# Windowed attention: the products with the values of one group are made together one group later, the output projection in half portions, TensorE held to the written order

## The chip, the cores and the metric

The kernel runs on one core of one Trainium2 chip. The metric is device time in microseconds (us) of one execution. The time before is the median of three runs; a profiled execution of the same kernel gives the trace that every reading below comes from. A difference under 0.3% (about 9 us) can't be told from no change here.

## What is computed

Two layers over 1024 latent tokens with 256 context tokens ahead of them, model width 1024. Layer 0 mixes tokens by two recurrent head groups, layer 1 by windowed attention; each layer ends with an MLP. Only the attention of layer 1 is touched by the change:

```python
def window_attention(q, k, v, k_c, v_c, sink):
    # q: 16 heads x 1024 x 64; k, v: 4 heads x 1024 x 64; k_c, v_c: 4 heads x 256 x 64
    ...
    s_loc = jnp.einsum('bkgnqd,bkncd->bkgnqc', qb, kb) * scale   # 128 queries x 3 blocks of 128 keys, band of +-128
    s_ctx = jnp.einsum('bkgnqd,bkld->bkgnql', qb, k_c) * scale   # the same queries x 256 context keys
    m = max over s_loc, s_ctx and the head's sink
    e_loc, e_ctx = jnp.exp(s_loc - m), jnp.exp(s_ctx - m)
    denom = sum(e_loc) + sum(e_ctx) + jnp.exp(s_sink - m)
    return (e_loc @ vb + e_ctx @ v_c) / denom
...
y = merge_heads(window_attention(...)) @ od_w_out
x = layer_norm(alpha * x + gate * y)
```

## The kernel before

The attention of layer 1 is cut into 32 groups: 8 blocks of 128 queries (`n`) by 4 key heads (`g`), with the 4 query heads of a key head worked on together. A group has `nk` blocks of 128 keys: 3 of the window and 2 of the context (at `n` = 0 and 7 one less). The closures of `group(n, g)` are its steps:

- `scores(i)`, i = 0 to 3, one query head: five matmuls into a score tile (`pS`, 2 buffers), then VectorE takes the maximum (`tensor_reduce`), scales it (`tensor_scalar`), and ScalarE makes the exponentials `E` (6 buffers) with their sum.
- `turn(kk)`, one block of keys: TensorE transposes that block of the four `E` into `pE` (2 buffers), ScalarE (VectorE for kk = 2) copies it to `Et`.
- `pv(kk)`: the product of that `Et` with 64 columns of the values, summed over kk in `pO` (1 buffer). The stationary side has 64 columns, and the two halves of `pO`'s partitions are written in turn.
- `dens()`: one over the denominators, and GpSimd's diagonal tiles `dg` from them. `end()`: a product of `dg` with ones in `pO`'s other half (so that every row gets its denominator), then VectorE and ScalarE make `yf`, and from it `yh` and `yl`, the two parts in which the output is kept.

Beside that runs `rest`, a chain of generators: after every second block of queries, `residual` multiplies the output of 256 tokens by the output weights (`w_out_steps`: 8 steps, each 24 matmuls into `pW` with one weight tile `w`), adds it to the residual stream and makes the layer norm. A `w` is made by `wsplit`: a load of 512 KB, a rounding copy on ScalarE (`hi`), a subtraction on GpSimd (`lo`); the pool `wg` holds 5 of them. `adv(rest, 1)` asks for one step.

A scheduler sets the order on each engine from the written order and a model of times. It may move an instruction ahead of others that are written earlier; once the program is built, every engine works strictly in the order it was given.

The loop over the groups, in which group u+1's scores are made during group u:

Of the kernel before, what the change touches and what calls it, by code (L numbers as in the profile page):

```python
# [9 lines left out]
F32 = mybir.dt.float32  # L10
# [9 lines left out]
P = 128  # L20
KT = 8
T = 1280
NT = 10
# [6 lines left out]
def chunk_of(t):  # L30
    return 0 if t < 2 else (1 if t < 6 else 2)
# [3 lines left out]
def backbone(ctx: ExitStack, tc: tile.TileContext, xT, cin, wmod, bmod, lng, lnb, w1, w2,  # L35
             wfm, wlr, wv, theta, gkw, gkb, normg, wo0, wq, wkv, sink, wo1, cst, rst, rope, out,
             stop=None, dbg=None):
    nc = tc.nc
# [3 lines left out]
            kw["reuse_waits"] = "tile"  # L42
        return tc.tile_pool(**kw)

    V, S, G, TE, SY = nc.vector, nc.scalar, nc.gpsimd, nc.tensor, nc.sync

    cp = ctx.enter_context(pool(name="cp", bufs=1))
    cp.tile([P, 16], F32, tag="pad", name="pad")
# [8 lines left out]
    def nm(s):  # L57
        uid[0] += 1
        return f"{s}_{uid[0]}"
# [104 lines left out]
    def chain(*gens):  # L164
        for g_ in gens:
            yield from g_
# [9 lines left out]
    def reserve(pool, tags):  # L176

        for tag, shape, dt, nb in tags:
            for _ in range(nb):
                pool.tile([P] + shape, dt, tag=tag, name=nm(tag), bufs=nb)  # L180
# [18 lines left out]
    def mm3(pt, wh, wl, xh, xl, start, stop):  # L199
        TE.matmul(pt, lhsT=wh, rhs=xh, start=start, stop=False)  # L200
        TE.matmul(pt, lhsT=wh, rhs=xl, start=False, stop=False)  # L201
        TE.matmul(pt, lhsT=wl, rhs=xh, start=False, stop=stop)  # L202
# [19 lines left out]
    wp = es_b1.enter_context(pool(name="w_b1", bufs=3, side="right"))  # L222
# [99 lines left out]
    with es_b1:  # L322
# [20 lines left out]
        for q in range(4):  # L343
# [5 lines left out]
            for a in range(2):  # L349
                k = 2 * q + a  # L350
# [33 lines left out]
        E = {}  # L384
# [101 lines left out]
    wg = ctx.enter_context(pool(name="wg", bufs=5, side="right"))  # L486
    with pool(name="b2", bufs=1) as b2:
# [38 lines left out]
        order = [1, 0] + list(range(9, 1, -1))  # L526
# [7 lines left out]
        for oi, t in enumerate(order):  # L534
            ci = chunk_of(t)
            j = cj(ci)
# [143 lines left out]
        for _ in w_out_steps(*a):  # L680
            pass

    def w_out_steps(y, wsrc, wp, acc, l, j, pW, engs=(None, None), wnext=None):

        n = acc.shape[2]
        yh, yl = y
        for u in range(KT):
            wh, wl = [w.rearrange("p (k m) -> p k m", k=KT) for w in (wnext() if wnext else wsplit(wp, wsrc[u], engs[u % 2]))]
            pt = pW()
            for k in range(KT):  # L690
                xh, xl = [y_[k // 4][:, k % 4, :] if isinstance(y_, list) else y_[:, k, :] for y_ in (yh, yl)]
                mm3(pt[:, :n], wh[:, k, :], wl[:, k, :], xh, xl, k == 0, k == KT - 1)
            V.scalar_tensor_tensor(acc[:, u, :], pt[:, :n], gta[:, l, 0, u, j:j + 1], acc[:, u, :],  # L693
                                   op0=ALU.mult, op1=ALU.add)
            yield
# [15 lines left out]
    with pool(name="b3", bufs=1) as b3:  # L711
# [28 lines left out]
        order = [wfm] + [wfm] + [wo0, wfm] * 3 + [wo0, wo0]  # L740
# [497 lines left out]
    yall = [hy.tile([P, KT, 512], F32R, tag=f"y{i}", name=f"y{i}") for i in "hl"]  # L1238
    with pool(name="p2", bufs=1) as p2:
        vts = {}  # L1240
        reserve(p2, [("E", [640], F32, 6), ("vc", [256], F32, 2), ("vl", [256], F32, 4)])

        def get_v(t):
            if t not in vts:
# [9 lines left out]
        def residual(y, t, ci):  # L1254
            o0 = (t - 1) * P - CH[ci][0]
            if o0 == 0:
                accs[ci] = new_acc(acp, ci)
            asl = accs[ci][:, :, o0:o0 + 256]
            G.tensor_copy(asl[:, 0, 0:1], first[0])
            SY.dma_start(asl, xd[ci][:, :, o0:o0 + 256])  # L1260
            yield from w_out_steps(y, wo1, wg, asl, 1, 0, pW if t < NT - 1 else pE, (None, None) if t < NT - 1 else (None, V))
            if t in (NT - 3, NT - 1):
                make_h(accs[1][:, :, o0:o0 + 256], 1, 1, 0, *[y_[:, :, o0:o0 + 256] for y_ in yall], p2, "ln_q", 1)
            if t < NT - 1:
                yield from layer_norm_steps(asl, 1, 0, p2, "ln_s", "ln_q", 1, False, pW, 512)
# [5 lines left out]
        def group(n, g):  # L1271
# [10 lines left out]
            def scores(i):  # L1282
                if i == 0:
                    if g == 0:
                        for k_ in keys:
                            get_v(k_)
                    if g % 2 == 0:
                        qts[0] = (p2 if g else kp).tile([P, 2, 4, P], F32R, tag="qt", name=nm("qt"), bufs=1)
                        for a in range(2):
                            G.dma_start(qts[0][:, a], qTd[n][g // 2][a].rearrange("l d j c -> (l d) j c"))  # L1290
                    st_["q"] = qts[0]
                    st_["sm"] = kp.tile([P, 4, 4], F32, tag="sm", name=nm("sm"), bufs=4)
                sm_ = st_["sm"]
                h = 4 * g + i
                q_ = st_["q"][:, h % 2, h % 8 // 2, :]
                S_ = pS()
                sl_ = S_[:, 512 - L:512]
                sc_ = S_[:, 512:768]
                for w_ in range(2):
                    TE.matmul(sl_, lhsT=q_, rhs=kall[:, w_, g, k0:k0 + L], start=(w_ == 0), stop=False)  # L1300
                if len(mk) == 2:
                    TE.matmul(sl_.rearrange("p (b c) -> p b c", c=P)[:, 0::2, :], lhsT=identb, rhs=wmask, start=False,
                              stop=True)
                else:
                    w_, o_ = mk[0]
                    TE.matmul(sl_[:, o_:o_ + P], lhsT=identb, rhs=wmask[:, w_, :], start=False, stop=True)
                for w_ in range(2):
                    TE.matmul(sc_, lhsT=q_, rhs=kall[:, w_, g, 0:256], start=(w_ == 0), stop=(w_ == 1))
                sall = S_[:, 512 - L:768]
                V.tensor_reduce(sm_[:, 0, i:i + 1], sall, AX.X, ALU.max)  # L1310
                V.tensor_scalar(sm_[:, 1, i:i + 1], sm_[:, 0, i:i + 1], -0.125, nsnk[:, h:h + 1],
                                op0=ALU.mult, op1=ALU.min)
                E_ = p2.tile([P, 640], F32, tag="E", name=nm("E"), bufs=6)
                S.activation(E_[:, :256 + L], sall, AF.Exp, scale=0.125, bias=sm_[:, 1, i:i + 1],
                             accum_out=sm_[:, 3, i:i + 1])
                Es.append(E_)

            def dens():
                sm_ = st_["sm"]
                first[0] = sm_[:, 1, 0:1]  # L1320
                V.tensor_tensor(sm_[:, 2, :], snk[:, 4 * g:4 * g + 4], sm_[:, 1, :], ALU.add)
                S.activation(sm_[:, 2, :], sm_[:, 2, :], AF.Exp)
                V.tensor_tensor(sm_[:, 2, :], sm_[:, 2, :], sm_[:, 3, :], ALU.add)
                V.reciprocal(sm_[:, 2, :], sm_[:, 2, :])
                dg = st_["dg"] = p2.tile([P, 4, P], F32, tag="dg", name=nm("dg"), bufs=1)
                for i in range(4):
                    G.tensor_scalar(dg[:, i, :], ident, sm_[:, 2, i:i + 1], 1.0, op0=ALU.mult, op1=ALU.mult)
                st_["po"] = pO()

            def turn(kk):  # L1330
                pe = pE()
                for i in range(4):
                    TE.transpose(pe[:, i * P:(i + 1) * P], Es[i][:, kk * P:(kk + 1) * P], ident)
                Et = p2.tile([P, 512], F32, tag="Et", name=nm("Et"), bufs=3)
                if kk == 2:
                    V.tensor_copy(Et, pe)
                else:
                    S.copy(Et, pe)
                st_[kk] = Et

            def pv(kk):
                po = st_["po"]
                vt = get_v(keys[kk])[:, 64 * g:64 * g + 64]
                Ev = st_[kk].rearrange("p (j a c) -> p a j c", a=2, j=2)
                for a2 in range(2):
                    TE.matmul(po[64 * a2:64 * a2 + 64, 0:256].rearrange("p (j c) -> p j c", j=2), lhsT=vt,
                              rhs=Ev[:, a2], start=(kk == 0), stop=(kk == len(keys) - 1))
# [12 lines left out]

            return len(keys), scores, dens, turn, pv, end

        SLOTS = (1, 2)
        todo = [(n, g) for n in range(8) for g in range(4)]
        nxt = group(*todo[0])
        for i in range(4):
            nxt[1](i)
        for u, (n, g) in enumerate(todo):
            nk, _, dens, turn, pv, end = nxt
            nxt = group(*todo[u + 1]) if u + 1 < len(todo) else None  # L1370
            sc = [lambda i=i, f=nxt[1]: f(i) for i in range(4)] if nxt else []
            dens()
            for kk in range(nk):
                turn(kk)
                if sc:
                    sc.pop(0)()
                if kk > 0:
                    pv(kk - 1)
                if kk in SLOTS:
                    adv(rest, 1)  # L1380
            for f in sc:
                f()
            pv(nk - 1)
            end()
            if g == 3 and n % 2 == 1:
                rest = chain(rest, residual([y_[:, :, (n % 4) * P - P:(n % 4) * P + P] for y_ in yall], n + 2, chunk_of(n + 2)))
        adv(rest, 1000)
    if stop == "x3":
        for ci in (1, 2):
# [134 lines left out]
```

## Time and profile before

| | |
|---|---|
| median of 3 runs | 3017.8 us (3013.01 to 3021.67) |
| profiled execution | 3027.12 us, of which span 3025.3 us |
| TensorE busy | 2922.6 us (97%) |
| VectorE, ScalarE, GpSimd busy | 1525.4, 976.4, 809.9 us |
| attention stage | about 1882 to 2256 us of the span |

The span runs from the first to the last instruction. A matmul's busy time includes its way through the array, so that a busy TensorE is not one at its peak: what a piece of work costs there is read from the distance between starts. PE is TensorE, PEld its weight loads, DVE VectorE, ACT ScalarE, POOL GpSimd. L1333 is a line of the kernel: in the attention L1300 to L1308 are the matmuls of the scores, L1310 and L1311 VectorE's work on them, L1314 the exponentials, L1333 the transposes, L1338 and L1336 the copies to `Et`, L1346 the products with the values, L1352 the denominators' product; L188 and L189 are the two halves of `wsplit`, L200 to L202 the matmuls of the projection.

### The profile page before, as it was taken

Reading aid. Unit: us, or ns where it says so; the run is one execution under the profiler, and the core shown is the slowest. Engines: PE = TensorE matmul, PEld = TensorE weight load, DVE = VectorE, ACT = ScalarE, POOL = GpSimd, SP = SyncE. Lnnn points to the kernel's source line nnn. Section 1 sums busy time; section 2 is a strip of 40 time slices with the busy share of each in tenths; the row PEclk is TensorE's granted clock in tenths of the full one; section 3 lists DMA queues with packets and bytes.
Section 4 is the critical chain, followed back from the end, with each engine's and each line's share of the span. In section 5 each row is a group of like instructions: output and inputs, shape, how many; then the busy total and the mean of one; then the engine's idle time right before and its main releaser. Section 6 shows DMA issues by size and latency. Waiting matters only on the chain. (4 is left out here: it accounts for less than half of the span.)

```text
span 3025.3 us, 43318 instructions
## 1 busy us (share of the span) xinstructions
PE 2922.6 (97%) x17856; PEld 2386.6 (79%) x17856; DVE 1525.4 (50%) x2489; ACT 976.4 (32%) x1617; POOL 809.9 (27%) x609
## 2 busy tenths in 40 slices
PE   7989998999999999999999999999999999999997
PEld 4766788888888888888888777677678888888886
DVE  3654477777434333433334654666775333333445
ACT  4534344444211111111111442556653221112113
POOL 3120145445211111111111342244344221122121
PEclk9999999999999999999999999999999999999999
DMA  7278575663222222221100166222221111111111
GB/s 254 96 229 254 185 260 193 202 202 112 78 70 79 68 80 67 80 67 49 42 29 15 67 200 179 75 79 74 71 70 63 56 56 36 49 56 50 36 41 56
DMA packets 164261, 304.52 MB, mean 101 GB/s; under 512 B 13504, under 2 KB 90560, under 8 KB 163552
## 3 DMA queue, kind: packets, MB, share of 16 engines
q1 hardware_dynamic: 145648, 272.91, 28.0%
q0 software_dynamic: 6480, 16.26, 1.9%
q10 hardware_dynamic: 11936, 12.59, 1.4%
q8 instruction: 140, 2.29, 0.3%
q14 instruction: 57, 0.47, 0.0%
HBM read 257.67 MB, written 44.04 MB: 100 GB/s over the span
## 5 line engine op out<-in xcount | busy, mean ns | idle before, releaser
L189 POOL TENSOR_TENSOR w<-raw,w 128x1024 fp32r<-128x1024 f32 x210 | 507.4, 2424 | 1683.4 <-ACT w L188 1642.9
L999 DVE SCALAR_TENSOR_TENSOR acc<-k,gta,acc 128x512 f32<-128x512 f32 (+1 forms) x704 | 443.2, 648 | 831.0 <-PE k L202 823.7
L200 PE MATMUL k<-hh,w 128*128 128x256 f32 (+1 forms) x1632 | 556.9, 342 | 5.1 <-DVE hh L196 3.4
L201 PE MATMUL k<-hl,w 128*128 128x256 f32 (+1 forms) x1632 | 555.0, 340 | 4.0 <-POOL hl L197 3.4
L202 PE MATMUL k<-hh,w 128*128 128x256 f32 (+1 forms) x1632 | 551.1, 338 | 0.2 <-POOL w L189 0.2
L188 ACT CAST w<-raw 128x1024 fp32r<-128x1024 f32 x260 | 269.5, 1048 | 822.5 <-PE k L202 540.3
L200 PE MATMUL k<-uh,w 128*128 128x512 f32 (+1 forms) x1408 | 503.0, 357 | 4.2 <-DVE acc L999 4.0
L201 PE MATMUL k<-ul,w 128*128 128x512 f32 (+1 forms) x1408 | 495.4, 352 | 0.0
L202 PE MATMUL k<-uh,w 128*128 128x512 f32 (+1 forms) x1408 | 494.8, 351 | 0.0
L200 PEld LDWEIGHTS k<-hh,w 128*128 128x128 f32 x1632 | 312.5, 192 | 54.9 <-issue 16.3
L201 PEld LDWEIGHTS k<-hl,w 128*128 128x128 f32 x1632 | 312.5, 192 | 44.8 <-issue 7.6
L202 PEld LDWEIGHTS k<-hh,w 128*128 128x128 f32 x1632 | 312.4, 191 | 34.4 <-issue 2.8
L200 PEld LDWEIGHTS k<-uh,w 128*128 128x128 f32 x1408 | 266.5, 189 | 55.4 <-issue 14.2
L981 ACT ACTIVATE r<-k 128x512 f32<-128x512 f32 (+1 forms) x176 | 90.9, 516 | 649.7 <-PE k L202 649.0
L202 PEld LDWEIGHTS k<-uh,w 128*128 128x128 f32 x1408 | 266.7, 189 | 36.7 <-issue 1.0
L201 PEld LDWEIGHTS k<-ul,w 128*128 128x128 f32 x1408 | 266.7, 189 | 35.3 <-issue 0.8
L200 PE MATMUL k<-yh,w 128*128 128x256 f32 (+1 forms) x544 | 183.9, 338 | 10.1 <-DVE acc L693 10.1
L201 PE MATMUL k<-yl,w 128*128 128x256 f32 (+1 forms) x544 | 181.2, 333 | 0.0
L202 PE MATMUL k<-yh,w 128*128 128x256 f32 (+1 forms) x544 | 181.1, 333 | 0.0
L984 DVE TENSOR_TENSOR r<-r 128x1024 f32<-128x1024 f32 (+1 forms) x88 | 113.9, 1295 | 127.7 <-ACT uh L983 127.4
L673 POOL TENSOR_SCALAR acc<-acc,lg_t,lb_t 128x256 f32<-128x256 f32 x124 | 103.1, 847 | 116.1 <-DVE acc L667 46.8
L200 PEld LDWEIGHTS k<-yh,w 128*128 128x128 f32 x544 | 106.5, 196 | 22.6 <-DVE acc L693 11.5
(300 smaller groups left out, 4419.2 us busy)
## 6 DMA issues: line engine op xcount, KB each, us to landing
raw<-in_w SPq DMA_DIRECT2D x128, 512.0 KB, 3.4
raw<-in_wo SPq DMA_DIRECT2D x72, 512.0 KB, 3.5
raw<-in_wmod SPq DMA_DIRECT2D x128, 256.0 KB, 2.7
raw<-in_wfm SPq DMA_DIRECT2D x48, 512.0 KB, 5.6
raw<-in_wmod SPq DMA_DIRECT2D x32, 512.0 KB, 4.2
kt<-kd SPq DMA_DIRECT2D x20, 512.0 KB, 6.0
qt<-qT POOLq DMA_DIRECT2D x32, 256.0 KB, 4.3
qT<-qT ACTq DMA_DIRECT2D x30, 256.0 KB, 3.7
```

The source lines that it names most:

```text
L188: S.copy(hi, raw)
L189: (eng or G).tensor_tensor(lo, raw, hi.bitcast(F32), ALU.subtract)
L200: TE.matmul(pt, lhsT=wh, rhs=xh, start=start, stop=False)
L201: TE.matmul(pt, lhsT=wh, rhs=xl, start=False, stop=False)
L202: TE.matmul(pt, lhsT=wl, rhs=xh, start=False, stop=stop)
L673: G.tensor_scalar(acc[:, k, :], acc[:, k, :], lg_t[:, l, s, k:k + 1], lb_t[:, l, s, k:k + 1], op0=ALU.mult, op1=ALU.add)
L981: S.activation(rf[:, i, :n], pts[i][:, :n], AF.Relu)
L984: V.tensor_tensor(rf[:, :, :n], rf[:, :, :n], rf[:, :, :n], ALU.mult)
L999: V.scalar_tensor_tensor(a_, pt[:, :n], gta[:, l, 1, m, cj(ci):cj(ci) + 1], a_, op0=ALU.mult, op1=ALU.add)
```

## The change

The loop is written in another order. In group u, after `turn(2)`, `finish` makes all products with the values of group u-1 in a row and its `end()`. For that the transposed `E` of a whole group are kept: the first four blocks in one tile of the pool `wg`, under the weights' tag `w` (8 KB each, one of the 5 buffers), the fifth in a tile of its own. `E` has 7 buffers instead of 6. A step of the output projection is cut after 12 of its 24 matmuls (`halves`, not for the last 256 tokens), and three steps are asked for in a group instead of two. In the loop each instruction of TensorE gets a dependency, without a wait, on the one written before it (`Tensor.kept`), so that the scheduler keeps the written order there. Outside the loop no instruction moves but a few at its seams.

```diff
+    class Tensor:
+        kept = False
+        last = None
+        def put(self, ins):
+            ins = getattr(ins, "ins", ins)
+            if self.kept and self.last is not None:
+                tc.add_manual_dep(ins, self.last.name, mybir.DependencyInfo(
+                    mybir.DependencyClass.NoSync, mybir.DependencyReason.DATA), reason="order")
+            self.last = ins if self.kept else None
+            return ins
...
                 mm3(pt[:, :n], wh[:, k, :], wl[:, k, :], xh, xl, k == 0, k == KT - 1)
+                if halves and k == 3:
+                    yield
...
-                st_["po"] = pO()
...
-                Et = p2.tile([P, 512], F32, tag="Et", name=nm("Et"), bufs=3)
+                if kk == 0:
+                    st_["Et"] = wg.tile([P, 4, 512], F32, tag="w", name=nm("Et"))
+                Et = st_["Et"][:, kk, :] if kk < 4 else p2.tile([P, 512], F32, tag="Et", name=nm("Et"), bufs=1)
...
+        def finish(n, g, unit):
+            nonlocal rest
+            nk, _, _, _, pv, end = unit
+            for kk in range(nk):
+                pv(kk)
+            end()
+            if g == 3 and n % 2 == 1:
+                rest = chain(rest, residual(...))
...
-            dens()
             for kk in range(nk):
                 turn(kk)
-                if sc:
-                    sc.pop(0)()
-                if kk > 0:
-                    pv(kk - 1)
-                if kk in SLOTS:
-                    adv(rest, 1)
-            for f in sc:
-                f()
-            pv(nk - 1)
-            end()
+                if nxt and kk < 4:
+                    nxt[1](kk)
+                if kk == 2:
+                    if prev:
+                        finish(*prev)
+                    dens()
+                if kk < 3:
+                    adv(rest, 1)
```

TensorE at the passage from one group to the next, before. `E_16972` to `E_17089` are the four exponentials of the coming group, the last one made from the last scores; `pO` is the product with the values, `pS` the scores of the group after.

```order
L1346 MATMUL pO_2358_16955<-Et_17079,v_15754 64x256 x2
L1333 MATMUL pE_2387_17121<-ident,E_16972 128x128
L1333 MATMUL pE_2387_17121<-ident,E_16989 128x128
L1333 MATMUL pE_2387_17121<-ident,E_17039 128x128
L1300 MATMUL pS_2392_17134<-kall,qt_17130 128x384 x2
L1302 LDWEIGHTS identb
L1302 MATMUL pS_2392_17134<-wmask,identb 128x2x128
L1308 MATMUL pS_2392_17134<-kall,qt_17130 128x256
L1333 MATMUL pE_2387_17121<-ident,E_17089 128x128
```

The same place after (all of TensorE's lines are now L61 and L64, those of the helper). `E_16828` is the exponential made from the last scores, which stand five rows ahead of this piece; the first three rows are transposes of the older group's last block.

```order
L64 MATMUL pE_2318_16830<-ident,E_16601 128x128
L64 MATMUL pE_2318_16830<-ident,E_16617 128x128
L64 MATMUL pE_2318_16830<-ident,E_16681 128x128
L64 MATMUL pE_2320_16837<-ident,E_16709 128x128
L64 MATMUL pE_2320_16837<-ident,E_16738 128x128
L64 MATMUL pE_2320_16837<-ident,E_16772 128x128
L64 MATMUL pE_2320_16837<-ident,E_16828 128x128
L61 MATMUL pS_2323_16845<-kall,qt_16697 128x384 x2
L61 LDWEIGHTS identb
L61 MATMUL pS_2323_16845<-wmask,identb 128x2x128
L61 MATMUL pS_2323_16845<-kall,qt_16697 128x256 x2
L61 MATMUL pW_2327_16860<-yh,w_16857 128x256
```

Before, a product with the values, four transposes, another product, three transposes of the coming group and most of the next scores stood between the last scores and the transpose of what is made from them (`E_17089`). Now seven transposes stand there and nothing else, and the next scores stand behind.

ScalarE around the rounding copy of a weight tile, before; `w_17215` is used by TensorE while the group after that of the exponentials beside it is transposed, `w_17814` many groups later.

```order
L1338 COPY Et_16814<-pE_2336_16809 128x512
L1358 CAST yh<-yf_16773 128x2x128
L1314 ACTIVATE E_16824,sm_16798<-pS_2338_16816,sm_16798 128x640
L188 CAST w_17215<-raw_17213 128x1024
L188 CAST w_17814<-raw_17812 128x1024
L1338 COPY Et_16914<-pE_2350_16909 128x512
```

The same after; `w_16857` is the weight tile of the projection row with which TensorE's piece above ends, `Et_16842` the copy of the transposes ahead of it.

```order
L1337 ACTIVATE E_16828,sm_16700<-pS_2316_16820,sm_16700 128x640
L1345 ACTIVATE sm_16700<-sm_16700 128x4
L1362 COPY Et_16842<-pE_2320_16837 128x512
L209 CAST w_16857<-raw_16855 128x1024
L209 CAST w_16947<-raw_16945 128x1024
L1337 ACTIVATE E_16853,sm_16844<-pS_2323_16845,sm_16844 128x640
```

The rounding copy has moved from more than a group ahead of its use to directly ahead of it, behind the copy of the same group's first transposes.

More of the change, by code (lines that the diff above doesn't have):

```diff
@@ L43, in pool, with matmul, transpose @@
         return tc.tile_pool(**kw)
-    V, S, G, TE, SY = nc.vector, nc.scalar, nc.gpsimd, nc.tensor, nc.sync
+    V, S, G, SY = nc.vector, nc.scalar, nc.gpsimd, nc.sync
+    class Tensor:
[8 more added lines that the diff above has]
+            return ins
+        def matmul(self, *a, **kw):
+            return self.put(nc.tensor.matmul(*a, **kw))
+        def transpose(self, *a, **kw):
+            return self.put(nc.tensor.transpose(*a, **kw))
+    TE = Tensor()
     cp = ctx.enter_context(pool(name="cp", bufs=1))
@@ L681, in w_out, with w_out_steps @@
             pass
-    def w_out_steps(y, wsrc, wp, acc, l, j, pW, engs=(None, None), wnext=None):
+    def w_out_steps(y, wsrc, wp, acc, l, j, pW, engs=(None, None), wnext=None, halves=False):
         n = acc.shape[2]
@@ L1240, in backbone @@
         vts = {}
-        reserve(p2, [("E", [640], F32, 6), ("vc", [256], F32, 2), ("vl", [256], F32, 4)])
+        reserve(p2, [("E", [640], F32, 7), ("vc", [256], F32, 2), ("vl", [256], F32, 4)])
         def get_v(t):
@@ L1260, in residual @@
             SY.dma_start(asl, xd[ci][:, :, o0:o0 + 256])
-            yield from w_out_steps(y, wo1, wg, asl, 1, 0, pW if t < NT - 1 else pE, (None, None) if t < NT - 1 else (None, V))
+            yield from w_out_steps(y, wo1, wg, asl, 1, 0, pW if t < NT - 1 else pE, (None, None) if t < NT - 1 else (None, V), halves=t < NT - 1)
             if t in (NT - 3, NT - 1):
@@ L1312, in scores @@
                                 op0=ALU.mult, op1=ALU.min)
-                E_ = p2.tile([P, 640], F32, tag="E", name=nm("E"), bufs=6)
+                E_ = p2.tile([P, 640], F32, tag="E", name=nm("E"), bufs=7)
                 S.activation(E_[:, :256 + L], sall, AF.Exp, scale=0.125, bias=sm_[:, 1, i:i + 1],
@@ L1341, in pv @@
             def pv(kk):
+                if kk == 0:
+                    st_["po"] = pO()
                 po = st_["po"]
@@ L1361, in group @@
             return len(keys), scores, dens, turn, pv, end
-        SLOTS = (1, 2)
         todo = [(n, g) for n in range(8) for g in range(4)]
+        def finish(n, g, unit):
[5 more added lines that the diff above has]
+            if g == 3 and n % 2 == 1:
+                rest = chain(rest, residual([y_[:, :, (n % 4) * P - P:(n % 4) * P + P] for y_ in yall], n + 2, chunk_of(n + 2)))
         nxt = group(*todo[0])
@@ L1367, in backbone @@
             nxt[1](i)
+        prev = None
+        TE.kept = True
         for u, (n, g) in enumerate(todo):
-            nk, _, dens, turn, pv, end = nxt
+            cur = nxt
+            nk, _, dens, turn, pv, end = cur
             nxt = group(*todo[u + 1]) if u + 1 < len(todo) else None
-            sc = [lambda i=i, f=nxt[1]: f(i) for i in range(4)] if nxt else []
-            dens()
             for kk in range(nk):
                 turn(kk)
-                if sc:
-                    sc.pop(0)()
-                if kk > 0:
-                    pv(kk - 1)
-                if kk in SLOTS:
-                    adv(rest, 1)
-            for f in sc:
-                f()
-            pv(nk - 1)
-            end()
-            if g == 3 and n % 2 == 1:
-                rest = chain(rest, residual([y_[:, :, (n % 4) * P - P:(n % 4) * P + P] for y_ in yall], n + 2, chunk_of(n + 2)))
+                if nxt and kk < 4:
[5 more added lines that the diff above has]
+                if kk < 3:
+                    adv(rest, 1)
+            prev = (n, g, cur)
+        finish(*prev)
+        TE.kept = False
         adv(rest, 1000)
```

## The prediction

> **What bounds the kernel now.** I read the page's head first, then the attention stage by itself, then who waits there.
>
> ```profile
> span 3025.3 us, 43318 instructions
> PE 2922.6 (97%) x17856; PEld 2386.6 (79%) x17856; DVE 1525.4 (50%) x2489; ACT 976.4 (32%) x1617; POOL 809.9 (27%) x609
> ```
>
> ```profile
> 1882.00:2256.00 374.00, 365.55 (x2589) 257.30 (x2588) 251.93 (x576) 228.01 (x497) 140.94 (x207) 0.99 0.25 79
> ```
>
> The second row is the stage: length, then busy time of TensorE, its weight loads, VectorE, ScalarE and GpSimd, then the granted clock. TensorE bounds it, busy in 365.6 of 374 us at clock 0.99. What it waits for, from the first group's end on, in full:
>
> ```profile
> PE pO L1346 <- ACT Et L1338: 1.7, 2, 1.0
> PE pO L1346 <- DVE yf L1356: 0.4, 2, 0.3
> PE pE L1333 <- ACT E L1314: 0.3, 1, 0.3
> ```
>
> So 2.4 us in 353: nobody is waited for. Whatever shortens TensorE's stream shortens the stage, and whatever makes it wait lengthens it by the whole wait. The order was bent around waits; that is what the change gives up.
>
> **Gain: fewer passages into and out of the products with the values.** 608 matmuls of L1346 are 152 blocks of four, in 32 groups.
>
> ```profile
> L1333 PE MATMUL pE<-ident,E 128*128 128x128 f32 x608 | 105.8, 286 | 0.4 <-ACT E L1314 0.3
> L1346 PE MATMUL pO<-Et,v 128*64 128x256 f32 x608 | 105.4, 406 | 4.7 <-DMA v<-vT 2.6 <-ACT Et L1338 1.7 <-DVE yf L1356 0.4
> ```
>
> What a passage costs is the distance of starts in the timeline:
>
> ```profile
> 1902.45 1.08 PE L1346 MATMUL pO<-Et,v 128*64 128x256 f32 x8
> ...
> 2067.42 0.48 PE L1308 MATMUL pS<-kall,qt 128*128 128x256 f32 x2
> 2067.74 0.49 PE L1333 MATMUL pE<-ident,E 128*128 128x128 f32 x3
> ...
> 2069.16 0.48 PE L1308 MATMUL pS<-kall,qt 128*128 128x256 f32 x2
> 2069.57 0.65 PE L1346 MATMUL pO<-Et,v 128*64 128x256 f32 x4
> 2070.15 0.66 PE L1333 MATMUL pE<-ident,E 128*128 128x128 f32 x4
> 2070.74 0.65 PE L1346 MATMUL pO<-Et,v 128*64 128x256 f32 x4
> ...
> 2198.13 0.60 PE L1333 MATMUL pE<-ident,E 128*128 128x128 f32 x4
> 2198.49 0.59 PE L1300 MATMUL pS<-kall,qt 128*128 128x384 f32 x2
> 2198.92 0.28 PE L1302 MATMUL pS<-wmask,identb 128*128 128x256 bf16 x1
> 2198.96 0.48 PE L1308 MATMUL pS<-kall,qt 128*128 128x256 f32 x2
> 2199.37 0.65 PE L1346 MATMUL pO<-Et,v 128*64 128x256 f32 x4
> ```
>
> Four such matmuls more in a row cost 1.08 - 0.65 = 0.43 us; followed by transposes they take 0.58 (2069.57 to 2070.15): 0.15 on the way out. On the way in, the last pair of scores takes 0.41 ahead of them and 0.32 ahead of transposes: 0.09; four transposes take 0.59 ahead of them and 0.36 ahead of scores: 0.23. A block that joins another saves 0.24 to 0.38. After the change a group has one run instead of 5 (or 4): 152 - 32 = 120 blocks join, 29 to 46 us. More blocks follow scores or projection than transposes, so I take 0.29: **-35 us**.
>
> [...]
>
> **Loss 1: the first transposes of a group wait for its last exponential.** In the new order the last scores, the transposes of the fifth block and then the coming group's transposes follow each other; the fourth of these reads the exponential of those last scores. That chain, as it ran:
>
> ```profile
> 2073.92 0.48 PE L1308 MATMUL pS<-kall,qt 128*128 128x256 f32 x2
> 2074.44 0.82 DVE L1310 TENSOR_REDUCE sm<-pS 128x1 f32<-128x640 f32 x1 [0.49 <-PE pS L1308]
> 2075.30 0.21 DVE L1311 TENSOR_SCALAR sm<-sm,nsnk 128x1 f32<-128x1 f32 x1
> 2076.07 0.79 ACT L1314 ACTIVATE E<-pS,sm 128x640 f32<-128x640 f32 x1
> 2076.74 0.20 ACT L1314 ACTIVATION_READ_ACCUMULATOR E<-pS,sm 128x1 f32 x1
> ```
>
> From the start of the last pair: 0.52 to the maximum, 0.82 + 0.04 + 0.21 on VectorE, about 0.1 to ScalarE, 0.87 there, 0.1 back: 2.65 us. TensorE has 0.32 (pair) + 0.36 (fifth block's transposes) + three of four transposes, 0.3: 1.0 us. It stands for 1.65. Other work of VectorE or ScalarE falls into the chain: `yl` (0.43), ordered between maximum and scale in groups without projection, and the copies to `Et`:
>
> ```profile
> L1338 ACT COPY Et<-pE 128x512 f32<-128x512 f32 x120 | 69.1, 585 | 30.6 <-PE pE L1333 30.3
> L1359 DVE TENSOR_TENSOR yl<-yf,yh 128x256 fp32r<-128x256 f32 x31 | 13.3, 428 | 0.0
> ```
>
> So 1.65 to 2.1 a group. Nothing excludes that some of it overlaps better, so the lower end is 1.4. 31 passages: 43 to 65 us; I take 1.8, near the upper end since both engines have such work in every group: **+56 us**. Queued behind the waiting transpose are the next scores, whose maximum and exponential start later by as much.
>
> **Loss 2: weights made only when they are needed.** `wg` has 5 buffers. Before, all were weights, and ScalarE's rounding copy ran as soon as a buffer came free:
>
> ```profile
> L188 ACT CAST w<-raw 128x1024 fp32r<-128x1024 f32 x26 | 27.3, 1049 | 58.9 <-PE pW L202 52.0 <-issue 5.9 <-DMA raw<-in_wo 1.0
> L189 POOL TENSOR_TENSOR w<-raw,w 128x1024 fp32r<-128x1024 f32 x25 | 61.0, 2441 | 81.2 <-ACT w L188 81.2
> ```
>
> It waited 52 us for TensorE to give buffers back, and no projection matmul stands in the list of TensorE's waits: the weights were ready early. Now transposed exponentials take two of the five in turn, and the copy stands on ScalarE behind the copy of the group's first `Et`, which itself needs the transpose that loss 1 holds up. Counted from that last exponential: TensorE needs 0.1 + 0.1 for the transpose and 0.80 for the scores (2198.49 to 2199.37, less the way in), then wants the weight, at 1.0. ScalarE: 0.1 + 0.35 until the transposes have landed, 0.585 + 1.05: weight there at 2.1; TensorE stands 1.1. The third matmul needs GpSimd's half, 2.44 later, and TensorE gets there 0.23 after the first: it stands 2.2 more. Three weights serve two groups; of them one pays 3.3, one is split right behind it and pays nothing, one is wanted later in its group, behind a half portion (12 matmuls, 1.4), transposes and scores, and pays about 0.65. 8 x 3.95 = **+32 us** for the 24 weights inside the loop. Ends: 14 (GpSimd's half hidden: 8 x 1.75) and 49 (the second weight waits for GpSimd's half too: 8 x 6.15). Weight loads keep two raw buffers ahead and cost nothing; if that cover went, each late one would add up to its 3.5 us of landing.
>
> **Loss 3: scores wait for a score buffer.** `pS` has two. In groups without projection nothing but a block of transposes stands between scores, so the third scores come 0.80 + 0.36 + 0.80 + 0.36 = 2.3 us after the first began, and the first's buffer is free after 0.80 of matmuls and the chain's 0.04 + 0.82 + 0.04 + 0.21 + 0.1 + 0.87: 2.9. 0.6 each, some 16 groups: **+10 us**, from 3 (if the copies fall favourably) to 14.
>
> **Small parts.** The projection in halves makes some 24 more passages of TensorE; nearest are the 0.09 to 0.23 above, 2 to 6: **+4**. At the start the first product comes a group later, and its wait for the values goes:
>
> ```profile
> PE pO L1346 <- DMA v<-vT: 2.6, 1, 2.6
> ```
>
> **-3.** Seven `E`: the eighth exponential reuses the first's buffer, free when the fifth block's transposes end, 0.7 after the last scores begin and so ahead of the exponential. `pO` is asked for a group after its last reader. `dg` has a whole group until it is used. The query loads on GpSimd's queue and the weight loads on SP's keep their order and lead. All of these at nothing. At the end up to two steps of a layer norm more are left over, beside the last projection's 192 matmuls; zero, at most 3.
>
> **Sum**: -35 + 56 + 32 + 10 + 4 - 3 = +64 us, against the profiled execution's 3027.1: 3091. The median of the runs lies 9.3 below that execution, so 3082.
>
> **Rivals.**
>
> *The passages saved outweigh the waits (faster).* Speaks for it that the gain is read from starts, and would be 46 at most. It decides from the wait of loss 1: with weights ready early it must be under (35 - 10 - 4 + 3) / 31 = 0.8 us a group. At 0.3 us, with the whole gain and 5 of loss 3 and small parts: -46 + 9 + 5, 2986. Against it stands the chain: 2.65 us of fixed work cannot hide under 1.0 us of transposes.
>
> *Weights come early after all.* GpSimd is busy 141 of 374 us and ScalarE 228, so there is room; losses 1 and 3 stay: -35 + 56 + 10 + 1 gives 3050. Against it stands the built order of ScalarE, which puts the copy behind the transposes.
>
> *The clock falls.* TensorE now pauses twice a group. The granted clock did fall in the stretch before the stage's first products:
>
> ```profile
> 1820.00:1825.00 5.00, 3.05 (x17) 2.29 (x16) 2.49 (x4) 0.59 (x1) 0.00 (x0) 1.00 1.13 314
> 1885.00:1890.00 5.00, 2.40 (x12) 1.97 (x11) 2.41 (x6) 2.98 (x6) 5.00 (x4) 0.64 0.89 271
> ```
>
> At 3.05 of 5 us busy it was 1.00, at 2.40 it was 0.64. I expect 8 of 10.5 us busy, with pauses of 2 us. Should a tenth of the stage's 330 us of work fall to 0.64, it adds 33 / 0.64 - 33 = 19: 3101, and a third 3144. [...]
>
> **How the numbers follow.** Forecast of waits that outweigh: 0.78, with 3045 to 3110. Weights early: 0.11, inside the range at 3050. Clock falls: 0.06, upper edge. Waits hidden, faster: 0.03; in parallel halves of the product, 33 lower than the forecast, 3049 and still slower: 0.02. The gain at 46 with each loss at its low end (43, 14, 3, 2, -3) makes +13, the gain at 29 with each at its high end (65, 49, 14, 6, -3) +102; all at one end is unlikely, and I take +22 to +92, from 3040 to 3110. Within 0.3% (what can't be told from no change): 0.03, the low ends together, out of the forecast's 0.78. Faster 0.03, same 0.03, slower 0.94.
>
> **What would show it.** In the trace after: a run of 20 products with the values in each group and about 32 passages out of them; in the stage TensorE waiting for the exponentials' line 30 times or so for 1.5 to 2 us each; matmuls into `pW` waiting for ScalarE's and GpSimd's halves of the weights, 16 to 24 times, some 30 us together; groups of 10 to 10.6 us without projection. The stage would be about 438 us instead of 374, with clock 0.99. The prediction is wrong if the transposes wait under 1 us a group, if the weights are there in time, or if anything outside the stage moves by more than 5 us.

## The result, and the profile after

The changed kernel took 3109.97 us (median of 4 runs, 3109.74 to 3112.1) beside 3018.64 us of the kernel before on the same chip: 1.0306 times as long, with a 95% interval of 1.0288 to 1.0324. That is 91 us more, where the forecast was 64 more; 3110 is the upper end of its range.

The page's head of the changed kernel, and three stretches: ahead of the attention stage, the stage, behind it. A row has its length, the busy time of TensorE, its weight loads, VectorE, ScalarE and GpSimd, then the granted clock (the share of full speed at which TensorE was let run).

```profile
span 3110.3 us, 43244 instructions
PE 2917.6 (94%) x17856; PEld 2417.1 (78%) x17856; DVE 1531.6 (49%) x2489; ACT 983.2 (32%) x1617; POOL 807.4 (26%) x609
```

```profile
0.00:1874.00 1874.00, 1799.77 (x11450) 1491.95 (x11451) 936.63 (x1476) 564.84 (x864) 477.16 (x301) 0.99 0.40 126
1874.00:2336.00 462.00, 368.65 (x2599) 293.41 (x2596) 256.29 (x570) 234.85 (x494) 140.59 (x208) 0.91 0.20 60
2336.00:3110.00 774.00, 749.22 (x3810) 631.73 (x3810) 338.66 (x444) 183.52 (x259) 189.64 (x100) 0.99 0.16 52
```

TensorE has as much busy time as before in the stage (368.7 us against 365.6) and 88 us more of stage to have it in; and the clock, 0.99 before, is 0.91. From the first scores to the last row of products with `dg` the stage took 372.3 us before and takes 459.6 now: +87. This distance is the measure of the stage below. The code ahead of the stage is the same in all kernels of this study, and it ended anywhere between 1869 and 1884 us in their profiles, so differences of a few us there mean nothing. Stage, waits and clock of a kernel are all read from one profiled execution of it.

Who is waited for in the stage, from the rows of TensorE's weight loads (total us, times, longest; they are nearer than the matmuls' rows to what the distances of starts show, as with the eighth transpose below: 1.53 us in its matmul's row, 1.82 by starts):

```profile
PEld pE L64 <- ACT E L1337: 59.4, 36, 3.6
PEld pW L61 <- POOL w L210: 28.7, 16, 5.4
...
PEld pS L61 <- ACT E L1337: 11.7, 12, 2.2
PEld pW L61 <- ACT w L209: 9.1, 8, 1.2
```

Transposes wait for exponentials (59), projection matmuls for the two halves of their weights (29 + 9), scores for a buffer that an exponential frees (12). In the stage before, the matmuls' rows of all waits came to 8 us together.

The gain is there too. A whole group without projection, in the timeline after, at clock 1.00:

```profile
1936.20 2.38 PE L61 MATMUL pO<-Et,v 128*64 128x256 f32 x20
1938.41 0.60 PE L61 MATMUL pO<-dg,ones_c 128*64 128x256 f32 x4
...
1940.15 0.93 PE L64 MATMUL pE<-ident,E 128*128 128x128 f32 x7
1942.60 0.33 PE L64 MATMUL pE<-ident,E 128*128 128x128 f32 x1 [1.53 <-ACT E L1337]
...
1945.85 0.62 PE L61 MATMUL pS<-kall,qt 128*128 128x384 f32 x2 [0.63 <-ACT E L1337]
...
1946.76 2.38 PE L61 MATMUL pO<-Et,v 128*64 128x256 f32 x20
```

and one of before:

```profile
1959.13 0.60 PE L1352 MATMUL pO<-dg,ones_c 128*64 128x256 f32 x4
...
1968.24 0.60 PE L1352 MATMUL pO<-dg,ones_c 128*64 128x256 f32 x4
```

Two runs of 20 products are 10.56 us apart; a group took 9.11 before. Seven transposes need 7 x 0.09 = 0.63, so that the eighth stands for 1942.60 - 1940.15 - 0.63 = 1.82, and the third scores for about 0.85. Without the two waits the group would be 7.9 long, 1.2 less than before, or some 38 us over 31 groups.

The groups with projection look different; a piece of one:

```profile
1987.94 0.93 PE L64 MATMUL pE<-ident,E 128*128 128x128 f32 x7
1990.18 0.33 PE L64 MATMUL pE<-ident,E 128*128 128x128 f32 x1 [1.32 <-ACT E L1337]
...
1992.13 0.39 PE L61 MATMUL pW<-yh,w 128*128 128x256 f32 x1 [0.91 <-ACT w L209]
1992.35 0.28 PE L61 MATMUL pW<-yl,w 128*128 128x256 f32 x1
1994.56 0.79 PE L61 MATMUL pW<-yh,w 128*128 128x256 f32 x2 [1.93 <-POOL w L210]
...
1996.86 1.05 PE L64 MATMUL pE<-ident,E 128*128 128x128 f32 x4
1997.57 0.99 PE L61 MATMUL pS<-kall,qt 128*128 128x384 f32 x2
```

Three pauses, 1.3, 0.9 and 1.9 us, fall within 6 us, one chain: the transpose waits for the exponential, the weight's copy for the copy of what is transposed, the subtraction for that copy. Behind them four transposes take 1.05 where they took 0.60 to 0.66. The granted clock by stretches says why (length, busy time of the five, clock):

```profile
1928.60:1932.00 3.40, 1.82 (x16) 1.43 (x14) 2.13 (x6) 2.40 (x6) 2.43 (x6) 1.00 0.20 40
1932.00:1935.40 3.40, 2.75 (x20) 2.19 (x21) 2.54 (x6) 2.11 (x5) 0.00 (x0) 1.00 0.40 119
1987.00:1996.00 9.00, 4.83 (x30) 3.88 (x29) 3.60 (x10) 5.41 (x10) 3.84 (x2) 0.85 0.05 5
1996.00:1999.40 3.40, 3.40 (x16) 3.09 (x16) 0.14 (x1) 0.58 (x1) 0.83 (x1) 0.50 0.76 257
```

Around the single pause of the first row the clock held (first two rows); after the three it was halved. Summed over stretches of 2 us, busy time times (1 - clock), the stage lost 4 us of TensorE's work to the clock before and 36 after. That is the term which the forecast's sum did not have. By the stretches at half clock, some 21 of the 36 lie behind eight such clusters of pauses, 3 behind one weight for which TensorE stood 5.4 us, and 13 behind single waits for an exponential: clusters are the larger part, and not the whole.

### The profile page after: what moved, and what is told of

Read it like the earlier page. It is cut to its first block, busy times and chain, and to the rows that moved or that the text cites. A ratio compares the mean times of both kernels' runs of the same rounds, so it can differ in the third digit from the quotient of the medians.

```text
span 3110.3 us, 43244 instructions
## 1 busy us (share of the span) xinstructions
PE 2917.6 (94%) x17856; PEld 2417.1 (78%) x17856; DVE 1531.6 (49%) x2489; ACT 983.2 (32%) x1617; POOL 807.4 (26%) x609
## 5 line engine op out<-in xcount | busy, mean ns | idle before, releaser
L61 PE MATMUL k<-hh,w 128*128 128x256 f32 (+1 forms) x3264 | 826.5, 339 | 5.2 <-DVE hh L217 3.4
L61 PE MATMUL k<-uh,w 128*128 128x512 f32 (+1 forms) x2816 | 769.7, 354 | 3.8 <-DVE acc L1022 3.7
L61 PEld LDWEIGHTS k<-hh,w 128*128 128x128 f32 x3264 | 568.8, 191 | 87.1 <-issue 17.1
L61 PEld LDWEIGHTS k<-uh,w 128*128 128x128 f32 x2816 | 500.6, 189 | 91.5 <-issue 15.0
L61 PE MATMUL k<-hl,w 128*128 128x256 f32 (+1 forms) x1632 | 554.6, 340 | 4.6 <-POOL hl L218 3.5
L61 PE MATMUL k<-ul,w 128*128 128x512 f32 (+1 forms) x1408 | 494.9, 351 | 0.0
L61 PEld LDWEIGHTS k<-hl,w 128*128 128x128 f32 x1632 | 311.7, 191 | 45.3 <-issue 7.4
L61 PEld LDWEIGHTS k<-ul,w 128*128 128x128 f32 x1408 | 266.1, 189 | 35.3 <-issue 0.8
L61 PE MATMUL k<-yh,w 128*128 128x256 f32 (+1 forms) x1088 | 269.7, 334 | 6.2 <-DVE acc L716 6.2
L61 PEld LDWEIGHTS k<-yh,w 128*128 128x128 f32 x1088 | 190.7, 195 | 28.4 <-DVE acc L716 7.4
L61 PE MATMUL k<-yl,w 128*128 128x256 f32 (+1 forms) x544 | 180.9, 333 | 0.7 <-POOL yl L967 0.7
L64 PE MATMUL pE<-ident,E 128*128 128x128 f32 x608 | 104.8, 297 | 50.4 <-ACT E L1337 50.4
L1333 DVE TENSOR_REDUCE sm<-pS 128x1 f32<-128x640 f32 (+1 forms) x128 | 100.9, 789 | 94.5 <-PE pS L61 93.9
L61 PE MATMUL pS<-kall,qt 128*128 128x256 f32 (+1 forms) x512 | 129.8, 367 | 9.2 <-ACT E L1337 8.9
L1337 ACT ACTIVATE E<-pS,sm 128x640 f32<-128x640 f32 (+1 forms) x128 | 98.2, 767 | 106.8 <-DVE sm L1334 104.4
L64 PEld LDWEIGHTS pE<-ident,E 128*128 128x128 f32 x608 | 77.1, 151 | 64.9 <-ACT E L1337 59.4
```

The lines of the kernel that those rows point to most:

```text
L61: return self.put(nc.tensor.matmul(*a, **kw))
L64: return self.put(nc.tensor.transpose(*a, **kw))
```

## The experiments

The theory after the result: the waits are as large as forecast, and what was missing (27 us) is the clock that falls behind the pauses. The main rival: the waits are larger than their rows and the clock costs nothing, since TensorE would only have waited longer. Each kernel was timed beside the kernel before on its chip, and the ratio is to that. In the table the waits are those of TensorE's weight loads in the stage; "lost" is the work lost to the clock, summed as above.

| kernel | time to before, 95% interval | stage us | exponentials / weights / scores waited for, us | lost us |
|---|---|---|---|---|
| changed kernel | 1.0306 (1.0288 to 1.0324) | 459.6 | 59 / 38 / 12 | 36 |
| weights ahead | 1.0142 (1.0120 to 1.0164) | 414.6 | 59 / 9 / 11 | 21 |
| products later | 1.0192 (1.0175 to 1.0209) | 430.9 | 19 / 43 / 19 | 27 |
| both | 1.0050 (1.0030 to 1.0070) | 385.0 | 19 / 12 / 19 | 14 |
| first pause filled | 1.0264 (1.0249 to 1.0279) | 449.0 | 18 / 38 / 16 | 18 |
| weights ahead, pause filled | 1.0147 (1.0122 to 1.0172) | 408.7 | 17 / 9 / 16 | 7 |
| both pauses filled | 1.0222 (1.0202 to 1.0242) | 437.6 | 18 / 19 / 16 | 6 |
| order free | 1.0087 (1.0058 to 1.0116) | 388.3 | 9 / 24 / 7 | 4 |
| kernel before, order kept | 1.0119 (1.0097 to 1.0141) | 406.8 | 5 / 0 / 12 | 10 |
| both, products split | 1.0024 (1.0010 to 1.0039) | 373.3 | 24 / 8 / 2 | 8 |

In rows with a pause filled, the filled part no longer counts as a wait; TensorE does idle work there. Where the order is free, the scheduler also moves matmuls of the last projection into the stage, so that its length says less. The profiled execution of the last row was 8 us under the median of its runs.

### Weights made a step ahead

Two weights are loaded and split ahead of a step's matmuls, so that one is always in hand for the next step:

```diff
+            ahead, srcs = [], iter(range(KT))
+            def wnext():
+                while len(ahead) < 2:
+                    ...
+                    ahead.append(wsplit(wg, wo1[u_]))
+                return ahead.pop(0)
-            yield from w_out_steps(y, wo1, wg, asl, ..., halves=t < NT - 1)
+            yield from w_out_steps(y, wo1, wg, asl, ..., halves=t < NT - 1, wnext=wnext if t < NT - 1 else None)
```

> The changed kernel with one addition: inside the loop the weights of the projection's next step are loaded and split one step ahead of their use (the projection of the last 256 tokens stays as it is). Theory A (waits and clock): the 38 us in which TensorE waits for weights fall to about 5, the 59 us for the exponentials stay, and without the long pauses at the weights the granted clock of the stage rises from 0.91 to 0.95 or more, which gives back some 15 us: 3110 - 33 - 15 = 3062 us. Rival B (waits alone; the lower clock costs nothing because it falls together with pauses): 3110 - 33 = 3077 us. Rival C (buffers short, the waits for weights only move): 3100 us or more.

Measured: 1.0142, 50 us less than the changed kernel. The waits of the weight loads:

```profile
PEld pE L64 <- ACT E L1348: 59.3, 36, 3.8
...
PEld pS L61 <- ACT E L1348: 11.1, 12, 2.2
PEld pW L61 <- POOL w L210: 7.5, 2, 5.4
```

The waits for weights fell by 29, the other two stayed within 0.6 us, and yet the stage became 45 us shorter. The 16 beyond the waits are about as many as the work lost to the clock fell (36 to 21). That is theory A's 48 us and not rival B's 33.

### The products behind the last scores

```diff
-                if kk == 2:
+                if kk == 3:
                     if prev:
                         finish(*prev)
                     dens()
```

> The changed kernel with the products with the values of the older group (finish, dens) moved from behind the third scores to behind the last ones, so that 2.7 us of them stand between the last scores and the transposes that need their exponential. Theory: the 59 us of waits for the exponentials fall to 10, but the four scores now follow each other with a block of transposes between, 1.16 us apart, against a chain of 2.9 us and two score buffers: the third and fourth wait 0.6 us each, 10 us become 30. Weights unchanged. 3110 - 49 + 20 = 3081 us. Rival (the chain hidden and the buffers hold): 3055 us. Rival (the wait was for something else): 3105 us or more.

Measured: 1.0192. With 24 matmuls between the last scores and the transpose of what is made from them, the first wait shrinks from 59 to 19 (the theory had 10):

```profile
PEld pW L61 <- POOL w L210: 32.1, 16, 5.4
PEld pS L61 <- ACT E L1337: 19.1, 23, 2.1
PEld pE L64 <- ACT E L1337: 18.8, 28, 1.4
```

The scores wait 7 us more and the weights 5 more, so 28 us net go with the waits, and the stage is 29 shorter. Here nothing beyond the waits shows, although the work lost to the clock fell by some 9.

### Both edits

> Both: weights one step ahead and the products behind the last scores. If the two losses are independent, their savings add: by theory A 3110 - 48 - 29 = 3033 us, with the clock near 0.97; by rival B (waits alone) 3048 us. If one had hidden the other, it stays above 3060 us.

Measured: 1.0050. The two savings, 1.64% and 1.14%, make 2.78%, and both together saved 2.56%, which the intervals allow: the waits have separate causes. 2.56% is 77 us, theory A's figure; rival B had 62.

### The first pause filled with idle work

To change the clock without the waits: 12 idle transposes ahead of each group's first transposes, while the exponential is made.

```diff
+                if kk == 0:
+                    for r in range(12):
+                        TE.transpose(pe[:, 3 * P:4 * P], Es[r % 3][:, 0:P], ident)
```

> The changed kernel with 12 more transposes, whose result is overwritten, ahead of the first transposes of each group: they need nothing that is late and take about 1.3 us of the pause of 1.3 to 1.6 us in which TensorE waits for the last exponential. No wait is removed in substance, only the pause is filled. Theory A (a lower clock after pauses costs time): the clock of the stage rises and the time falls by 5 to 20 us, to 3090 to 3105 us. Rival B (the clock costs nothing): 3110 to 3118 us.

Measured: 1.0264, 13 us less than the changed kernel with more work in it. Idle work makes nothing earlier, and VectorE, ScalarE and GpSimd have the same instructions in the same order in the stage as in the changed kernel; what differs is the clock, 0.96 over 1874 to 2336 us where it was 0.91. The intervals of the two kernels do not touch.

### Weights ahead, and the pause filled

> The kernel with weights one step ahead (ratio 1.014, clock in the stage 0.94) and the 12 more transposes in the pause ahead of each group's first transposes. Theory: with the weights early and this pause filled, no pause over 1 us is left in the loop, the clock of the stage goes to 0.98 and 8 to 15 us come back: ratio 1.009 to 1.0115. Rival (the clock's loss in that kernel comes from the stage's two ends, not from these pauses): ratio 1.014 to 1.016.

Measured: 1.0147, and 1.0142 without the filling: a miss. The work lost to the clock did fall from 21 to 7 us, so that the rival's reason, a loss at the stage's two ends, does not hold either; and the stage fell by 6, which the interval of the times (0.25% each way, 7 us) neither shows nor excludes. Part of what was won went into the scores' waits:

```profile
PEld pE L64 <- ACT E L1348: 17.4, 33, 2.5
PEld pS L61 <- ACT E L1348: 15.6, 16, 2.2
```

So lost work was not lost time one for one: 14 us of it won back went with 6 of stage here, 30 with 22 in the next run. Why the time did not fall here is the author's estimate, from the 4.5 us that the scores wait more: where TensorE waits for a chain on other engines anyway, a slower TensorE would only wait less. No run shows it.

### Both pauses filled

The direct test: idle work in the weights' pauses as well, in nine steps (the expectation says eight) whose weight comes late: `fills` is (2, 5), (0, 3, 6) and (0, 1, 4, 7) for the three projections.

```diff
+                if k == 0 and u in fills:
+                    for r in range(18):
+                        TE.matmul(pt[:, n:2 * n], lhsT=xh[:, 0:P], rhs=xh, start=True, stop=True)
```

> Both pauses filled: 12 idle transposes ahead of a group's first transposes, as in the run that filled that pause alone (1.0264, stage 449.2 us, clock 0.95, 18 us of TensorE's work lost to the clock), and 18 idle matmuls of 256 columns ahead of a projection step's first matmul in the eight steps whose weight comes late. The waits themselves stay: the weight is wanted and made at the same times. Theory (the pauses lower the clock, and part of what the clock takes lies on the path): the clock in the stage rises to 0.97 or more, the work lost to it falls from 18 to about 8 us, and half or so of that is seen in the time, 1.0240 to 1.0250 of before. If all of it were on the path, 1.023. Rival (the clock follows something else than these pauses, or costs no time): clock 0.95 and 1.0260 or more.

Measured: 1.0222, better than the theory's 1.0240 to 1.0250 and near the 1.023 for all of the lost work on the path; the interval reaches both. The other three engines keep the changed kernel's order here, too. The stage, and the stretch that ran at half clock in the changed kernel:

```profile
1874.00:2336.00 462.00, 422.10 (x3316) 349.56 (x3317) 271.62 (x588) 245.34 (x506) 157.29 (x220) 0.99 0.23 68
```

```profile
1987.00:1996.00 9.00, 8.00 (x64) 7.25 (x63) 2.54 (x7) 4.67 (x10) 4.73 (x2) 1.00 0.23 70
1996.00:1999.40 3.40, 3.40 (x32) 2.27 (x30) 2.29 (x5) 1.40 (x4) 0.00 (x0) 1.00 0.33 129
```

With the pauses filled the clock is 0.99, as before the change, and the stage 437.6: 22 us shorter for 30 us of lost work won back. What is left, 437.6 - 372.3 = 65 us, is the change at the clock of before, and the forecast's sum was 64. The rival, by which the clock costs nothing, is out: 1.0202 to 1.0242 here against 1.0288 to 1.0324 for the changed kernel.

### The order left to the scheduler

```diff
-        TE.kept = True
+        TE.kept = False
```

> The changed kernel with TensorE's written order no longer kept (the dependencies are left out, all else stays): the scheduler moves instructions into the waits and breaks the 32 runs of products with the values into 95. Theory: most of the 59 us of waits for the exponentials go (to 15), the 38 us for weights stay nearly (to 30), since the buffers are shared as before, 63 more passages cost 18 us, the clock gives back 15: about 85 us less waits and clock than after, plus 18: 3.06% over the kernel before becomes 0.8%, 3042 us at a time before of 3018. Rival (the kept order costs nothing, the other parts do): 3100 us.

Measured: 1.0087. The same program in the order that the scheduler chooses costs 66 us less:

```profile
PEld pW L61 <- POOL w L210: 22.7, 17, 3.7
...
PEld pE L64 <- ACT E L1337: 9.2, 25, 1.1
PEld pS L61 <- ACT E L1337: 7.2, 14, 1.7
```

The scheduler puts products between the scores and the transposes that wait for them: there are about 100 runs of products in the stage, not 32. It gives up most of the gain and most of the loss: the three waits make 40 us instead of 109, and 4 us of work are lost to the clock instead of 36.

### The kernel before, with its written order kept

> The kernel before with one addition: TensorE keeps the written order of the attention loop. Products with the values stay one block at a time, weights keep all five buffers. Theory: the last product of a group then waits for the copy of its transposes, 0.36 + 0.6 + 0.2 us after the transposes begin against one other product of 0.6, and the coming group's transposes for the last exponential, now covered by two products and the denominators (1.6 us of 2.65): about 1 us a group, 30 us, and little from the clock: 3018 + 35 = 3053 us. If the written order harms only together with the later products: 3018 to 3027 us.

Measured: 1.0119. The kernel before, too, loses by its written order, in another place:

```profile
PEld pO L61 <- ACT Et L1359: 42.3, 26, 2.8
```

There the last product of a group stands behind its own transposes with one other product between, and waits for the copy of these, as the theory had it; the second wait that it named, of the transposes for the last exponential, came to 5 us only. The order of before had been good since the scheduler had moved instructions; the wait for `Et`, 1.7 us in the trace of before, was hidden by that alone.

### Towards a version that keeps the gain

Both edits, and the first two blocks of products moved behind the second scores:

```diff
+        def start(n, g, unit):
+            for kk in range(2):
+                unit[4](kk)
...
-                if kk == 2:
+                if kk == 1 and prev:
+                    start(*prev)
+                if kk == 3:
```

> The kernel of weights one step ahead and products behind the last scores, with the first two blocks of products moved forward, behind the second scores: 64 runs instead of 32 (9 us more of passages), but 0.9 us more between the second and third scores. Theory: the waits of scores for their buffer fall from 19 to about 5 us, those of the transposes stay near 19, the clock gives back 5 to 8: 3037 - 14 + 9 - 7 = 3025 us on that chip (before 3024), ratio 1.000. Rival (the chain is only moved, the transposes wait for what the scores no longer wait): 3045 us.

Measured: 1.0024, between the theory (1.000) and the rival (some 1.007). The scores' waits went from 19 to 2 us as meant, those of the first transposes rose from 19 to 24, since fewer matmuls are left ahead of them. Then two versions with the order free, the first without the split:

> Weights made a step ahead, products behind the last scores, and the written order not enforced: the scheduler orders TensorE. Theory (each wait found is paid for by itself): the run with the order free alone took 1.0087 with 23 us of waits for weights and 9 for the first transposes; weights ahead take 15 of these, later products some 3: 1.002 to 1.004. Rival (the scheduler, given the freedom, breaks the long runs of products up again and its own choices make the rest): 1.006 to 1.009.

> As the run before it, with the first two blocks of products moved behind the second scores, and the order free. The same with the order enforced took 1.0024, with 24 us of waits of the first transposes and a clock of 0.98. Theory: the scheduler fills most of these with the scores that stand behind the waiting transpose: 0.997 to 1.000, the first version no slower than the kernel before. Rival: the order written out there is as good as the scheduler's, 1.001 to 1.004.

Measured: 0.9994 (0.9982 to 1.0006) and 0.9988 (0.9975 to 1.0000). The second lies in its theory's range (0.997 to 1.000); the first is better than its own (1.002 to 1.004), a miss: more went than the waits that its sum took away, and no run says what. What the split version still waits for in the stage is above all the first weight of each projection (matmuls' rows: total, times, longest):

```profile
PE pW L61 <- POOL w L210: 4.9, 3, 3.6
PE pO L61 <- POOL dg L1361: 2.1, 1, 2.1
```

So the last run made the first two weights one request earlier:

```diff
+            if t < NT - 1:
+                ahead += [wsplit(wg, wo1[next(srcs)]) for _ in range(2)]
+                yield
```

> As the run with products split and the order free, with the first two weights of each projection made one request ahead of its first step. In that run the first step of each projection still waited for GpSimd's half of its first weight: 0.32, 3.59 and 1.02 us, 4.9 together. Theory: these waits go and nothing takes their place, 0.9988 less 0.16%: 0.9965 to 0.9980, faster than the kernel before by little, but with an interval that leaves 1 out. Rival: the request that this uses shifts the projection by a third of a group, and the order that the scheduler then chooses has its own waits: 0.9985 to 1.001.

Measured: 0.9992 (0.9983 to 1.0000): the rival.

```profile
PE pW L61 <- POOL w L210: 3.9, 3, 2.3
PE pO L61 <- POOL dg L1364: 3.7, 2, 2.1
PE pE L61 <- DVE yl L1399: 2.9, 1, 2.9
```

GpSimd makes weights and `dg` one after the other; the weights came 1 us better and `dg` 1.6 worse, and a wait for `yl` is new. No version here is faster than the kernel before by what can be measured; the last three can't be told from it.

## Why the prediction was right and wrong

- **Bound.** TensorE's stream and its waits set the stage, as read: where a wait was taken away on the chip, the time followed (50 us, 45 of them in the stage, for 29 of waits and 15 of clock; 34, of them 29 in the stage, for 28 of waits).
- **Gain, 35 forecast.** About 38, by distances in groups without projection. The rate per block that joins a run (0.29 us) held. No run shows the 33 us that the chances have for parallel halves of the product: a run of 20 products takes 1938.41 - 1936.20 = 2.21 us, 0.44 for four where four more in a row took 0.43 before, so a block's two halves overlap no more than before.
- **Loss 1, 56 forecast.** 59, in 36 waits. The chain of 2.65 us, read from before, took about the same: 2.56 and 2.77 us from the last pair of scores to the transpose at 1990.18 and at 1942.60.
- **Loss 2, 32 forecast.** 38. Forecast pauses of a step were 1.1, 2.2 and 0.65; the timeline shows 0.9, 1.9 and 0.6 at their places; the rows count 8 waits for ScalarE's half and 16 for GpSimd's. One of the 16 is a single wait of 5.4 us, for a weight at 2226.86, which no term had; without it the sum is the forecast's.
- **Loss 3, 10 forecast.** 12.
- **Small parts.** The wait for the values is gone, as said. Behind the stage 5.7 us came on in the one profile of each, where at most 3 had been allowed; by the prediction's own list, more than 5 us outside the stage is a sign of being wrong. No run takes this apart.
- **The clock, left at 0.99.** This is the step that failed: "I expect 8 of 10.5 us busy, with pauses of 2 us", and from it that the clock would hold, with 0.06 for the rival. It averaged over a group, and counted nothing for pauses of 2 us. In groups with projection, loss 1 and loss 2 follow each other, as the forecast's own chain of loss 2 starts at the exponential for which loss 1 waits; 1987 to 1996 is 4.8 us busy of 9, little more than the share of the row at 0.64 that the prediction quoted (2.40 of 5). In its place the runs showed a clock of 0.91 and 36 us of lost work, 22 us of stage time that come back when the pauses are filled. The rival's lower case, a tenth of the work slowed, gave 19 us; by the times of the two kernels, filling the pauses shows 25 (some 17 to 33 by their intervals). The trace of before had the warning. The prediction set the clock of 1885 to 1890 beside the busy time of the same 5 us, but the clock fell behind a stretch, in which TensorE was busy for 1.60 us of 3.41:

```profile
1882.99:1886.40 3.41, 1.60 (x10) 1.03 (x9) 3.12 (x7) 2.11 (x3) 3.19 (x2) 1.00 0.70 256
1886.40:1889.81 3.41, 1.93 (x9) 1.74 (x10) 1.12 (x2) 1.94 (x5) 3.41 (x4) 0.50 0.88 255
```

- **Sum.** -38 for passages, +109 for waits less the 8 of before, +22 for the clock: +85 of the stage's 87. The forecast had the first two at +63, and so have the runs; that is in part luck, since the gain came 3 us larger and the waits 11, of which 8 had been there before.

So direction, places and prices of the waits were right, and the miss of 27 us is the clock's 22 to 25 plus a few us behind the stage.

## What to carry to other kernels

Price a wait twice: by its length, and by what TensorE's clock does behind it (here 109 us of waits, and 22 of clock). For the second, lay the forecast pauses on one time line and look at how little TensorE is busy in any 3.41 us of it, the step of the clock in these traces (half clock followed 1.54 and 1.60 us busy, full clock 1.92), not at the mean of a group; pauses with one cause came together here, 1.3, 0.9 and 1.9 us within 6 us. And when a reordering saves passages, look for what stood between a result and its use: a scheduler may have hidden 40 us of waits in an order that reads as wasteful.

## What the runs showed of the hardware

The granted clock fell to 0.50 behind pauses under 2 us (1.3, 0.9 and 1.9 us from 1989 to 1995, a single one of 1.8 at 1901), where the forecast had expected it to hold. In the changed kernel's stage it is 1.00 or 0.50, and all 16 falls to 0.50 begin whole multiples of a step of 3.413 us apart (130 steps from the first, at 1880.72, to the last, at 2324.45), and last one or two steps. Three steps of that kernel, each with the step behind it:

```profile
1897.79:1901.20 3.41, 1.60 (x14) 1.28 (x14) 2.07 (x7) 1.98 (x6) 1.05 (x4) 1.00 0.00 0
1901.20:1904.61 3.41, 3.41 (x18) 3.32 (x17) 1.64 (x4) 1.63 (x4) 0.00 (x0) 0.50 0.00 0
1928.51:1931.92 3.41, 1.92 (x16) 1.52 (x14) 2.22 (x6) 2.32 (x6) 2.52 (x6) 1.00 0.18 35
1931.92:1935.33 3.41, 2.68 (x20) 2.12 (x20) 2.47 (x6) 2.19 (x6) 0.00 (x0) 1.00 0.41 124
1989.95:1993.36 3.41, 1.54 (x8) 0.98 (x8) 1.38 (x4) 3.08 (x7) 1.20 (x1) 1.00 0.00 0
1993.36:1996.77 3.41, 2.21 (x10) 2.21 (x11) 0.00 (x0) 0.45 (x2) 3.41 (x2) 0.50 0.31 82
```

With 1.60 us of a step busy, around one pause of 1.8 us, the next step ran at half clock, and so it did with 1.54 us, in the cluster of three pauses; with 1.92 it held. In this stage half clock followed every step at full clock with up to 1.76 us busy but one (1.48, at 1918.27), and none with 1.82 or more. In other traces the line is not as sharp: with weights ahead a step with 1.88 us (1891.4 to 1894.8) was followed by half clock. In the changed kernel's stage a step at half clock was followed by a second one where TensorE was busy for 1.8 to 2.3 us of it, and by full clock where it was for 3.1 or more.

So a pause counted here by what it left busy within one step, which is how a single pause of 1.8 us was followed by a fall at 1901 (1.60 us busy) and one of 1.6 us was not at 1932 (1.92 us busy).

Idle transposes and idle matmuls on data at hand raised the clock of the stage (0.91 to 0.99 with both pauses filled), and where TensorE waited anyway no cost of them shows: the stage became 22 us shorter, 437.6 for 459.6.
